# Two layers of a bidirectional hybrid diffusion trunk on one core: the framework's scheduler orders each engine's instructions by its timeline simulation

## The chip, the cores and the metric

The kernel runs on one core of a Trainium2 chip (trn2). The metric is the device time of one launch in microseconds (us), the median of several runs. A core has TensorE (PE: matmuls; its weight loads are shown apart as PEld), VectorE (DVE), ScalarE (ACT), GpSimd (POOL) and SyncE (SP, which here issues the loads and stores). Each engine works through its own list of instructions in order; an instruction whose inputs are not there holds up all that stand behind it on its engine.

## The reference

One inference step of a trunk of two layers, model width 1024, on 128 context tokens and 512 latent tokens, all in fp32. Each layer is a half-step SwiGLU feed-forward, a token mixer and a second half-step feed-forward. Every part has an RMSNorm before it and shift, scale and gate vectors made from a conditioning vector (`mod_w`, nine blocks of 1024 x 1024 per layer):

```python
for i in range(DEPTH):
    m = (jax.nn.silu(cond) @ mod_w[i] + mod_b[i]).reshape(cond.shape[0], N_MOD, 1, D_MODEL)
    h = rmsnorm(x, norm_g[i, 0]) * (1.0 + m[:, 1]) + m[:, 0]
    x = x + 0.5 * m[:, 2] * swiglu(h, f1a[i], f1b[i])
    h = rmsnorm(x, norm_g[i, 1]) * (1.0 + m[:, 4]) + m[:, 3]
    if i % 2 == 0:
        y, s_a, s_b = mix_even(h, s_a, s_b, is_latent, even)
    else:
        y, s_a, s_b = mix_odd(h, s_a, s_b, odd)
    x = x + m[:, 5] * y
    h = rmsnorm(x, norm_g[i, 2]) * (1.0 + m[:, 7]) + m[:, 6]
    x = x + 0.5 * m[:, 8] * swiglu(h, f2a[i], f2b[i])
return rmsnorm(x, final_norm), new_states
```

`mix_even` is retention (four heads, chunks) beside a gated linear recurrence (RG-LRU); `mix_odd` is an S5 state-space layer beside RWKV-7. Each mixer runs over the tokens in both directions and has one input and one output projection.

## The kernel before, in words

The activations lie transposed: eight tiles `x[d]` of 128 channels by 640 tokens, worked on in two halves h of 320 columns (h=0 and h=1; h=1 holds 192 latent and 128 context columns, so what depends on the conditioning is two instructions there). A product in fp32 is made of three matmuls (`mm3`, L414 to L416) of a high and a low part: high by high, high weight by low data, low weight by high data. So every weight is loaded raw (L376, SP's queue), cast to its high part on ScalarE (`whi`, L377) and subtracted for its low part on VectorE or, for a few, GpSimd (`wlo`, L378). Two weights are in flight (`wp`, bufs=2).

The stages follow each other as f01, m0, f02, f11, m1, f12 and fin: feed-forward 1 of layer 0, its mixer, feed-forward 2, and so on.

- `ffn`: 22 blocks f of 128 hidden units, in groups of 7, 7, 6 and 2. For each block, `up` makes gate and value in four PSUM banks ("gu"), then L548 (Silu), L549 (product) and a split (L401, L402). After each of the first three groups an **output pass** follows: 16 accumulator groups of 21 or 18 matmuls (four weights times two channel tiles times two halves), in two PSUM banks ("acc"). `add_res` (L506, VectorE) adds each to `x` and so frees its bank: one instruction for h=0, two for h=1.
- The last group of two blocks is `last_pass`, a **joint** between stages: its releases (L506) go together with the next norm's squares (L441 to L445), its statistics (`stat`: L450 on TensorE, L453 to L460) and `apply`: L482 (VectorE), L487 (ScalarE, high part), L488 (VectorE, low part). The next stage's first matmuls read what L487 and L488 write; h=0 is applied inside `last_pass`, h=1 after the first h=0 matmuls of the next stage.
- `mod_steps` makes the modulation vectors: per block eight tiles `mw` of 128 x 1024 (L297, SP's queue), each multiplied into two sums on VectorE (L331 for the first tile, L333 for the others), and then small matmuls (L338). `extra()` puts two or three such steps after each hidden block and each weight of the output pass, above all in f01 and f11. Two first blocks are made on TensorE in the start (`first_mods`, L306 loads, L309 matmuls).
- `load_in_slots` (L385) loads the first weight of the next stage in four tiles; L392 and L393 split it on ScalarE and GpSimd.
- `mix0` has the recurrence's gate matmuls (L741) with their activations (L742, L744, L745, L756) beside retention heads; `mix1` has small matmuls of 64 columns (L1520) in chains with VectorE (L1594 to L1693), and projections (L1133 to L1410) between them.

The code's order is not the order on the engines. The program is written down as a whole, and on leaving the `TileContext` the framework's scheduler gives every engine its list. It keeps the dependences, and chooses among instructions that are ready by estimates of when each engine would be free and how long things take. With no argument it uses its default machine model for these estimates. The programs' names carry numbers (`mw_328`, `s_251`), by which one tile can be followed in both orders.

## Time and profile before

| what | us |
|---|---|
| median of 3 runs (lowest to highest) | 2984.92 (2982.17 to 2988.34) |
| profiled execution | 2976.69 |
| its span in the profile | 2974.9 |
| TensorE busy | 2824.3 |
| VectorE busy | 1774.9 |
| ScalarE busy | 970.5 |
| GpSimd busy | 267.1 |

The profiled execution is one run of its own, 1.8 us of it outside the span. Busy times are summed over the span. Windows give them stretch by stretch, with the number of instructions in parentheses; `PEclk` there is the clock granted to TensorE as a mean share of full speed, between its levels of 1.2 and 2.4 GHz. A wait is put down to the instruction that released it last.

### The profile page before, as it was taken

How to read it: one execution, taken by the hardware profiler on the slowest of the kernel's cores; microseconds unless marked ns; L12 is line 12 of the kernel's file. 1: busy time of each engine (PE TensorE's matmuls, PEld its weight loads, DVE VectorE, ACT ScalarE, POOL GpSimd, SP SyncE). 2: the span in 40 equal slices, each digit the busy share in tenths (PEclk: the TensorE clock that was granted, in tenths of full speed). 3: DMA queues.
4: the chain of work that ended last, by engine and by line, in shares of the span. 5: the costliest groups of instructions: out<-in, count | busy, mean ns of one | idle time of the engine just before them, and what ended most of it. 6: DMA issues, size and time to landing. Idle time of an engine off the chain costs nothing.

```text
span 2974.9 us, 60269 instructions
## 1 busy us (share of the span) xinstructions
PE 2824.3 (95%) x25764; PEld 2672.6 (90%) x25764; DVE 1774.9 (60%) x3717; ACT 970.5 (33%) x1825; POOL 267.1 (9%) x214
## 2 busy tenths in 40 slices
PE   6999999999999999999999999988888998999997
PEld 4999999887899999999999998986777888999997
DVE  7585773875795475558456556486665537233335
ACT  4222123574442122224122214235443424222123
POOL 2000000140010000010000002212222102000001
PEclk8999999999999999999999999998989999999999
DMA  7464543211223343443335443341000112222221
GB/s 280 133 199 134 185 149 119 93 43 57 90 78 96 102 123 109 152 152 103 113 120 159 131 156 103 116 149 40 5 5 13 45 44 71 66 84 66 84 71 64
DMA packets 121965, 305.27 MB, mean 103 GB/s; under 512 B 20832, under 2 KB 38880, under 8 KB 121568
## 3 DMA queue, kind: packets, MB, share of 16 engines
q1 hardware_dynamic: 121696, 301.42, 31.4%
q8 instruction: 202, 3.31, 0.5%
q14 instruction: 67, 0.55, 0.1%
HBM read 276.95 MB, written 24.42 MB: 101 GB/s over the span
## 4 chain that ended last, share of the span: by engine, by line
PE 80%; DVE 9%; issue 6%; ACT 2%; POOL 2%; DMA 1%; SPq 0%; DVEq 0%; ACTq 0%; POOLq 0%
PE gu L415 17%; PE gu L414 17%; PE gu L416 17%; PE acc L414 7%; PE acc L416 7%; PE acc L415 7%; PE m L1520 2%; PE acc L1520 1%; PE gu L1520 1%; DVE s L445 1%; DVE s L402 1%; DVE t L482 1%; PE gu L1184 1%; DVE s L506 1%; DVE ma L333 1%
## 5 line engine op out<-in xcount | busy, mean ns | idle before, releaser
L414 PE MATMUL gu<-s,whi 128*128 128x320 f32 x3344 | 1040.6, 312 | 1.3 <-ACT s L1270 1.3
L415 PE MATMUL gu<-s,whi 128*128 128x320 f32 x3344 | 1036.0, 310 | 0.0
L416 PE MATMUL gu<-s,wlo 128*128 128x320 f32 x3344 | 1035.5, 310 | 0.0
L414 PEld LDWEIGHTS gu<-s,whi 128*128 128x128 f32 x3344 | 628.7, 188 | 8.5 <-issue 3.4
L415 PEld LDWEIGHTS gu<-s,whi 128*128 128x128 f32 x3344 | 628.9, 188 | 3.3 <-issue 1.4
L416 PEld LDWEIGHTS gu<-s,wlo 128*128 128x128 f32 x3344 | 628.4, 188 | 0.9
L377 ACT CAST whi<-raw 128x1024 fp32r<-128x1024 f32 x322 | 316.8, 1000 | 788.6 <-PE acc L415 444.1
L414 PE MATMUL acc<-s,whi 128*128 128x320 f32 x1456 | 452.0, 310 | 6.3 <-DVE s L506 6.2
L416 PE MATMUL acc<-s,wlo 128*128 128x320 f32 x1456 | 451.2, 310 | 0.0
L415 PE MATMUL acc<-s,whi 128*128 128x320 f32 x1456 | 450.2, 309 | 0.0
L549 DVE TENSOR_TENSOR t<-t,gu 128x320 f32<-128x320 f32 x176 | 85.5, 487 | 521.9 <-PE gu L416 517.6
L378 DVE TENSOR_TENSOR wlo<-raw,whi 128x1024 fp32r<-128x1024 f32 (+2 forms) x298 | 342.5, 1164 | 61.6 <-ACT whi L377 61.6
L414 PEld LDWEIGHTS acc<-s,whi 128*128 128x128 f32 x1456 | 273.3, 188 | 11.7 <-DVE s L506 8.8
L333 DVE SCALAR_TENSOR_TENSOR ma<-mw,cT,ma 128x1024 f32<-128x1024 f32 x224 | 277.2, 1278 | 0.0
L416 PEld LDWEIGHTS acc<-s,wlo 128*128 128x128 f32 x1456 | 273.2, 188 | 0.8 <-DVE wlo L378 0.4
L415 PEld LDWEIGHTS acc<-s,whi 128*128 128x128 f32 x1456 | 273.3, 188 | 0.2 <-issue 0.2
L506 DVE SCALAR_TENSOR_TENSOR s<-acc,hg,s 128x320 f32<-128x320 f32 (+1 forms) x336 | 137.5, 435 | 218.5 <-PE acc L416 217.3
L401 ACT CAST s<-t 128x320 fp32r<-128x320 f32 x212 | 96.4, 455 | 323.5 <-DVE t L549 323.2
L548 ACT ACTIVATE t<-gu 128x320 f32<-128x320 f32 x176 | 76.7, 438 | 312.7 <-PE gu L416 312.6
L393 POOL TENSOR_TENSOR s<-s,s 128x512 fp32r<-128x512 f32 x28 | 38.9, 1418 | 1477.6 <-DVE s L402 1337.7
L402 DVE TENSOR_TENSOR s<-t,s 128x320 fp32r<-128x320 f32 x212 | 110.4, 521 | 33.8 <-ACT s L401 33.7
L414 PE MATMUL gu<-s,s 128*128 128x320 f32 x304 | 92.2, 338 | 30.3 <-ACT s L487 28.7
(426 smaller groups left out, 3519.7 us busy)
## 6 DMA issues: line engine op xcount, KB each, us to landing
raw<-w SPq DMA_DIRECT2D x224, 512.0 KB, 3.9
mw<-mod_w SPq DMA_DIRECT2D x144, 512.0 KB, 4.4
raw<-w_in SPq DMA_DIRECT2D x36, 512.0 KB, 3.6
raw<-w SPq DMA_DIRECT2D x32, 384.0 KB, 4.1
xs<-s SPq DMA_DIRECT2D x16, 320.0 KB, 2.2
s<-xs SPq DMA_DIRECT2D x16, 320.0 KB, 5.3
s<-w SPq DMA_DIRECT2D x16, 256.0 KB, 5.5
raw<-w SPq DMA_DIRECT2D x16, 256.0 KB, 3.7
```

The source lines that it names most:

```text
L333: DVE.scalar_tensor_tensor(acc[s], w, cT[:, k, s:s + 1], acc[s], ALU.mult, ALU.add)
L377: ACT.copy(hi[:, c], raw[:, :n])
L378: (eng or DVE).tensor_sub(lo[:, c], raw[:, :n], hi[:, c].bitcast(F32))
L401: (DVE.tensor_copy if eng is DVE else ACT.copy)(hi, src)
L402: DVE.tensor_sub(lo, src, hi.bitcast(F32))
L414: PE.matmul(ps, whi, xhi, start=start, stop=False)
L415: PE.matmul(ps, whi, xlo, start=False, stop=False)
L416: PE.matmul(ps, wlo, xhi, start=False, stop=stop)
L506: DVE.scalar_tensor_tensor(x[d][:, c0 + a:c0 + b], ps[:, a:b], g[:, d, s:s + 1], x[d][:, c0 + a:c0 + b], ALU.mult, ALU.add)
L548: ACT.activation(sg, pg, AF.Silu)
L549: DVE.tensor_mul(gf, sg, pu)
L1520: PE.matmul(out(rows[h]), lhs(rows[h], h), rhs(rows[h], h), start=i == 0, stop=i == len(terms) - 1, tile_position=(64 * h, 64 * h))
```

## The change

```diff
-    with tile.TileContext(nc) as tc:
+    with tile.TileContext(nc, schedule_with_timeline_sim=True) as tc:
         build(nc, tc, I, O)
```

The scheduler takes its estimates from the framework's timeline simulation and no longer from its default machine model. The same instructions result, with the same tiles, but for the table loads of ScalarE, which are put in wherever the next activation needs another table: 51 before, 67 now. On every engine the order differs in most stages; f12 is nearly the same. Three places:

SP's queue in the start, from the middle of the `first_mods` loads on (`mw` from `mod_w`: L306, and L297 for VectorE's mod work; `s_251` to `s_254`: the first feed-forward weight; `raw`: later weights). Before:

```order
L306 DMA mw_328<-mod_w 128x2x512
L385 DMA s_251<-w_1 128x512
L385 DMA s_252<-w_1 128x512
L385 DMA s_253<-w_1 128x512
L385 DMA s_254<-w_1 128x512
L306 DMA mw_334<-mod_w 128x2x512
L306 DMA mw_340<-mod_w 128x2x512
L306 DMA mw_346<-mod_w 128x2x512
L376 DMA raw_558<-w_1 128x1024
L376 DMA raw_562<-w_1 128x1024
L297 DMA mw_806<-mod_w 128x1024
L297 DMA mw_810<-mod_w 128x1024
```

Now:

```order
L306 DMA mw_322<-mod_w 128x2x512
L376 DMA raw_682<-w_1 128x1024
L306 DMA mw_328<-mod_w 128x2x512
L306 DMA mw_334<-mod_w 128x2x512
L376 DMA raw_686<-w_1 128x1024
L306 DMA mw_340<-mod_w 128x2x512
L306 DMA mw_346<-mod_w 128x2x512
L297 DMA mw_806<-mod_w 128x1024
L385 DMA s_251<-w_1 128x512
L385 DMA s_252<-w_1 128x512
L385 DMA s_253<-w_1 128x512
L385 DMA s_254<-w_1 128x512
```

The weight tiles of L385 went behind the last of the `first_mods` loads, two raw weights and one `mw` of L297.

VectorE near the end of the second output pass of f01 (`acc_…` are the accumulator groups, in order of their numbers; `ma` are the mod sums). Before:

```order
L378 TENSOR_TENSOR wlo_3360<-raw_3361,whi_3359 128x1024
L378 TENSOR_TENSOR wlo_3360<-raw_3365,whi_3359 128x1024
L506 SCALAR_TENSOR_TENSOR s_116<-acc_3265,hg_0_1432,s_116 128x320
L333 SCALAR_TENSOR_TENSOR ma_3126<-mw_3487,cT,ma_3126 128x1024
L435 SCALAR_TENSOR_TENSOR ns_2_7705<-mod_7_3014,vec 128x16
L506 SCALAR_TENSOR_TENSOR s_116<-acc_3288,hg_0_1432,s_116 128x192
L506 SCALAR_TENSOR_TENSOR s_116<-acc_3288,hg_0_1432,s_116 128x128
L506 SCALAR_TENSOR_TENSOR s_118<-acc_3312,hg_0_1432,s_118 128x320
L506 SCALAR_TENSOR_TENSOR s_118<-acc_3335,hg_0_1432,s_118 128x192
```

Now:

```order
L506 SCALAR_TENSOR_TENSOR s_116<-acc_3265,hg_0_1432,s_116 128x320
L333 SCALAR_TENSOR_TENSOR ma_3632<-mw_3769,cT,ma_3632 128x1024
L506 SCALAR_TENSOR_TENSOR s_116<-acc_3288,hg_0_1432,s_116 128x192
L506 SCALAR_TENSOR_TENSOR s_116<-acc_3288,hg_0_1432,s_116 128x128
L333 SCALAR_TENSOR_TENSOR ma_3631<-mw_3773,cT,ma_3631 128x1024
L333 SCALAR_TENSOR_TENSOR ma_3632<-mw_3773,cT,ma_3632 128x1024
L333 SCALAR_TENSOR_TENSOR ma_3631<-mw_3777,cT,ma_3631 128x1024
L333 SCALAR_TENSOR_TENSOR ma_3632<-mw_3777,cT,ma_3632 128x1024
L333 SCALAR_TENSOR_TENSOR ma_3631<-mw_3905,cT,ma_3631 128x1024
L506 SCALAR_TENSOR_TENSOR s_118<-acc_3312,hg_0_1432,s_118 128x320
```

Between the release of `acc_3288` and that of `acc_3312` stood nothing, and now five L333 stand there. From the pass's first L506 to its last there were 16 L333, 2 L331 and 8 L378 and are now 30, 4 and 6. In f01's first pass L333 went from 19 to 26, in f11's second from 12 to 26, in f02's third from 12 to 4.

VectorE at the joint of f02 and f11, from the statistics of h=0 (L458 to L460) to the first L488 of its apply (`s_7293` to `s_7307` are x, `wlo_13892` is the next stage's second weight, of which the two instructions come some 20 rows later in the order before). Before:

```order
L458 TENSOR_TENSOR t_13431<-t_13430 128x320
L506 SCALAR_TENSOR_TENSOR s_7301<-gu_13513,hg_2_9358,s_7301 128x192
L459 TENSOR_TENSOR t_13431<-t_13431,t_13429 128x320
L506 SCALAR_TENSOR_TENSOR s_7301<-gu_13513,hg_2_9358,s_7301 128x128
L460 SCALAR_TENSOR_TENSOR s_13314<-t_13431,t_13430 128x320
L506 SCALAR_TENSOR_TENSOR s_7303<-acc_13525,hg_2_9358,s_7303 128x192
L482 SCALAR_TENSOR_TENSOR t_13439<-s_7293,ns_0_13315,s_13314 128x320
L482 SCALAR_TENSOR_TENSOR t_13445<-s_7295,ns_0_13315,s_13314 128x320
L482 SCALAR_TENSOR_TENSOR t_13451<-s_7297,ns_0_13315,s_13314 128x320
L488 SCALAR_TENSOR_TENSOR s_13438<-t_13439,mod_0_3922,s_13437 128x320
```

Now:

```order
L506 SCALAR_TENSOR_TENSOR s_7307<-acc_13549,hg_2_9358,s_7307 128x128
L459 TENSOR_TENSOR t_13431<-t_13431,t_13429 128x320
L378 TENSOR_TENSOR wlo_13892<-raw_13893,whi_13891 128x1024
L460 SCALAR_TENSOR_TENSOR s_13314<-t_13431,t_13430 128x320
L378 TENSOR_TENSOR wlo_13892<-raw_13897,whi_13891 128x1024
L482 SCALAR_TENSOR_TENSOR t_13439<-s_7293,ns_0_13315,s_13314 128x320
L482 SCALAR_TENSOR_TENSOR t_13445<-s_7295,ns_0_13315,s_13314 128x320
L482 SCALAR_TENSOR_TENSOR t_13451<-s_7297,ns_0_13315,s_13314 128x320
L482 SCALAR_TENSOR_TENSOR t_13465<-s_7301,ns_0_13315,s_13314 128x320
L482 SCALAR_TENSOR_TENSOR t_13471<-s_7303,ns_0_13315,s_13314 128x320
L482 SCALAR_TENSOR_TENSOR t_13477<-s_7305,ns_0_13315,s_13314 128x320
L488 SCALAR_TENSOR_TENSOR s_13438<-t_13439,mod_0_3922,s_13437 128x320
```

Releases of h=1 and the two splits went ahead of the first L482, and three more L482 ahead of the first L488. The joints of f01 to m0 and f11 to m1 changed in the same way.

## Rows read from the trace of the kernel before

**Rows 1.** Page, its first line and section 1: span, busy us of each engine.

```profile
span 2974.9 us, 60269 instructions
...
PE 2824.3 (95%) x25764; PEld 2672.6 (90%) x25764; DVE 1774.9 (60%) x3717; ACT 970.5 (33%) x1825; POOL 267.1 (9%) x214
```

**Rows 2.** Windows: stretch, its us, busy (x instructions) per engine, PEclk, DMA share, GB/s.

```profile
300.00:350.00 50.00, 50.00 (x351) 49.11 (x350) 47.94 (x60) 9.20 (x12) 0.00 (x0) 1.00 0.70 217
600.00:650.00 50.00, 46.89 (x264) 41.25 (x262) 39.16 (x64) 36.95 (x63) 18.93 (x15) 0.97 0.12 43
2040.00:2100.00 60.00, 48.25 (x534) 30.67 (x534) 42.04 (x83) 34.88 (x59) 22.41 (x17) 0.83 0.10 29
2100.00:2200.00 100.00, 88.69 (x2366) 78.53 (x2364) 65.66 (x162) 42.65 (x111) 31.28 (x25) 0.86 0.02 4
2370.00:2460.00 90.00, 78.58 (x1244) 71.01 (x1241) 36.24 (x80) 24.79 (x60) 10.49 (x9) 0.95 0.24 75
2600.00:2650.00 50.00, 50.00 (x343) 50.00 (x342) 17.84 (x30) 8.74 (x11) 0.00 (x0) 1.00 0.24 82
```

**Rows 3.** Waits of TensorE, whole span: waiting line, releaser, total us, times, longest us.

```profile
PE gu L414 <- ACT s L487: 28.7, 13, 4.6
...
PE acc L414 <- DVE s L506: 7.0, 7, 2.3
...
PE m L741 <- ACT s L742: 5.3, 5, 2.6
```

**Rows 4.** Start: two windows, then SP's and TensorE's timeline (start us, us, instruction, wait).

```profile
30.00:35.00 5.00, 0.42 (x9) 0.09 (x1) 4.80 (x8) 3.49 (x8) 3.06 (x3) 1.00 1.05 386
35.00:40.00 5.00, 5.00 (x33) 2.23 (x34) 4.58 (x4) 1.31 (x4) 3.83 (x3) 0.66 0.96 381
...
23.13 1.88 SPq L385 DMA_DIRECT2D s<-w  x4
...
34.92 0.48 PE L414 MATMUL gu<-s,s 128*128 128x320 f32 x1 [4.58 <-ACT s L487]
```

**Rows 5.** Timeline of VectorE in the second output pass of f01.

```profile
316.01 1.22 DVE L378 TENSOR_TENSOR wlo<-raw,whi 128x1024 fp32r<-128x1024 f32 x1
317.14 0.55 DVE L506 SCALAR_TENSOR_TENSOR s<-acc,hg,s 128x320 f32<-128x320 f32 x1
317.61 0.95 DVE L378 TENSOR_TENSOR wlo<-raw,whi 128x768 fp32r<-128x768 f32 x1
...
320.70 1.42 DVE L331 TENSOR_SCALAR ma<-mw,cT 128x1024 f32<-128x1024 f32 x2 [0.39 <-PE m L338]
...
324.96 2.47 DVE L333 SCALAR_TENSOR_TENSOR ma<-mw,cT,ma 128x1024 f32<-128x1024 f32 x2
327.36 0.67 DVE L506 SCALAR_TENSOR_TENSOR s<-acc,hg,s 128x192 f32<-128x192 f32 x2
327.94 2.08 DVE L378 TENSOR_TENSOR wlo<-raw,whi 128x1024 fp32r<-128x1024 f32 x2
```

**Rows 6.** Joint of f02 and f11: timeline of VectorE; TensorE's waits, 1335 to 1400.

```profile
1343.86 2.03 DVE L482 SCALAR_TENSOR_TENSOR t<-s,ns,s 128x320 f32<-128x320 f32 x3
1345.81 0.54 DVE L488 SCALAR_TENSOR_TENSOR s<-t,mod,s 128x320 fp32r<-128x320 f32 x1
...
1353.50 1.23 DVE L378 TENSOR_TENSOR wlo<-raw,whi 128x1024 fp32r<-128x1024 f32 x1
...
PE gu L414 <- ACT s L487: 3.8, 2, 2.3
```

**Rows 7.** Timeline of ScalarE in mix0: a table load between two activations.

```profile
595.34 0.88 ACT L783 ACTIVATE t<-gu 64x320 f32<-64x320 f32 x2
596.24 1.28 ACT L756 ACT_TABLE_LOAD   x1
597.53 0.74 ACT L756 ACTIVATE s<-s 128x640 f32<-128x640 f32 x1
```

**Rows 8.** Waits of SP's queue, whole span.

```profile
SPq L297 <- DVE ma L333: 215.9, 94, 5.7
```

## The prediction

> **What bounds the kernel now.** I read the page's totals first. TensorE is busy 2824.3 of 2974.9 us and every other engine far less [rows 1], so the end moves only if TensorE comes to wait for longer, or shorter, than the 150.6 us for which it stands idle now. The profiled execution took 2976.7 us, 8.2 us under the median of 2984.9 us; I make the sum against the profiled one and add it to the median at the end. The windows say next where the idle time lies. In the feed-forward stages TensorE has none, 343 matmuls and 50.00 us in a window of 50, even where VectorE is busy 47.94 us of it [rows 2]. The idle time sits in the mixes (46.89 of 50 us at 600 us in mix0; 48.25 of 60, 88.69 of 100 and 78.58 of 90 us in three stretches of mix1), in the start, and at the joints between stages. The waits of TensorE name who ended it: at the joints and the start ScalarE's part of a norm's apply (L487, 28.7 us in 13 waits), in the feed-forward output passes VectorE's release of an accumulator (L506, 7.0 us), in mix0 the gate activations (L742, 5.3 us) [rows 3]. The change adds no arithmetic; it reorders. So I look for places where the new order puts other work of an in-order engine ahead of what TensorE needs next.
>
> **1. Start: +8 us.** All loads go through SP's one queue. From 30 to 35 us the DMA engines are full (share 1.05, 386 GB/s) and to 40 us nearly so (0.96) [rows 4]. In the new order six transfers of 128 x 1024 floats stand newly ahead of the first feed-forward weight tiles s_251 to s_254 (mw_334, mw_340, mw_346, raw_682, raw_686, mw_806): 3.15 MB by 0.386 MB per us is 8.1 us. These tiles were issued at 23.13 us before, and the first feed-forward matmul ran at 34.92 us, after a wait of 4.58 us for L487 and not for the weights [rows 4]. So the weights may have had up to a few us of slack, which gives a lower end of 4; the same weights still have to be split by ScalarE and GpSimd, and VectorE's mod work (L331, L378) now stands ahead of the norm's L482, which gives 12 at the upper end. I take 8, the queue's own arithmetic, since TensorE has nothing else to run there.
>
> **2. Output passes of f01 and f11: +13 us.** An output pass is 16 accumulator groups; 21 matmuls at 50 us per 343 [rows 2] make 3.07 us each, so 15 groups between VectorE's first and last release are 46.0 us. There are two accumulator banks, so VectorE may lag by about one group and no more. Back to back (start to start) VectorE takes 1.20 us for an L333 (two from 324.96 to 327.36), 0.47 us for an L506 of 320 columns (317.14 to 317.61), 0.58 us for the pair of 192 and 128 (327.36 to 327.94), 1.13 us for a wlo split of 1024 columns (316.01 to 317.14), and 0.71 us for an L331 (two in 1.42) [rows 5]. The splits of 768 columns I count like those of 1024. Before, the second pass of f01 holds 16 L333, 2 L331 and 8 splits between first and last L506: 19.2 + 1.4 + 9.0 + 8.4 for the releases, 38.0 us, and the trace shows TensorE full there [rows 2]. In the new order it holds 30 L333, 4 L331 and 6 splits: 36.0 + 2.8 + 6.8 + 8.4 = 54.0 us, 8.0 over the budget. The first pass of f01 and the second of f11 go to 26 L333 (from 19 and 12), 2 L331 and 6 splits: 31.2 + 1.4 + 6.8 + 8.4 = 47.8 us, 1.8 over each. That is 11.6 us by totals. It isn't spread evenly: in one place five L333 (6.0 us) stand between two releases, where a group takes 3.07, which costs up to 3 us on top each time; against that, work before the first and after the last release hides up to a group's time per pass. Bounds: 4 and 22. I take 13, near the totals, with a little for the bunches. Where the mod work leaves, nothing is saved, as TensorE was full there and VectorE had time to spare.
>
> **3. Joints between stages: +13 us.** At the joint f02 to f11 VectorE runs back to back from the last pass's releases through the statistics to the apply: three L482 from 1343.86, the first L488 at 1345.81, and the two wlo splits of the next weight only from 1353.50 on [rows 6]. TensorE waits 3.8 us for L487 in two waits there, the longest 2.3 us (so 1.5 and 2.3, h=0 and h=1) [rows 6]. The new order puts both splits (2.3 us) and the five remaining releases of h=1 (1.4 us) before the first L482, and six L482 (three more, 2.0 us at 0.65 each) before the first L488. The first L482 is 3.7 us later and the first L488 over 5 us later; the first L450 comes after fewer matmuls on TensorE, which gains nothing as VectorE is the one that is full. Of these 5 us, about 2.5 come back, since h=0 starting late takes away the wait of h=1, whose statistics are no later than before. That makes 2.5 us each at f01 to m0 and f11 to m1, and 3 at the two joints around f02. At f02 to f11 three L333 and two L331 stand besides among the apply of h=1 (about 5 us), so there nothing comes back: 5 us in all, 13 for the four. f12's joint has no split to move: 0. Bounds: 5 (everything made up while h=0 runs) and 20. One row raises the upper end: after the start's 4.58 us wait the granted clock of the next 5 us was 0.66 [rows 4], between the levels of 1.2 and 2.4 GHz; 0.34 of 5 us is 1.7 us. Four such waits would be another 7. The Trainium skill ("TensorE: Matmul & The Clock Gate", section "Why this matters for your kernels") says the same, that a gap between bursts of matmuls brings the half clock back; by it these 7 us belong in the sum, and it would be 38 where mine is 31.
>
> **4. mix0: -3 us.** TensorE's L741 groups stand further apart, with up to 32 projection matmuls between two of them where 15 stood, so the 5.3 us of waits for L742 [rows 3] can go. Against that ScalarE gets ten more table loads, because the square root (L756) is done per head and no longer per pair: 10 by 1.28 us = 12.8 us [rows 7] on an engine that is busy 36.95 of 50 us [rows 2]. In the row the load costs no more than its 1.28 us: the work before it ends at 596.22 and the next activation starts at 597.53. It can hide, as ScalarE has 13 us spare in each 50. The Trainium skill ("ScalarE: Activation LUTs", "What ACT_TABLE_LOAD costs") adds a drain and puts a switch at 2.66 us; by that figure, an estimate, ten cost 26.6 us, more than the spare time of two such windows, and this term would be about +5. The row shows no drain, so I keep -3; bounds -5 and +8.
>
> **5. mix1: 0.** Here nearly every row moves. Projection and key matmuls that filled TensorE between the links of the small-matmul chain are pulled ahead of early chains and missing in late ones, and six more table loads (7.7 us) come. No row prices this. The most that could be won is the idle time, 11.75 + 11.31 + 11.42 = 34.5 us in the three stretches [rows 2], and what the clocks of 0.83 and 0.86 cost there, 0.17 of 60 and 0.14 of 100 us, 24 us together. A loss of half that size is as easy. I put 0 with -25 and +20.
>
> The steady part of f12 and the end keep their order: 0. Sum: 8 + 13 + 13 - 3 + 0 = **+31 us**: 3007.7 for an execution like the profiled one, and 2984.9 + 31 = **3016 us** as a median.
>
> **Rivals.**
> *mix1 pays (faster).* The chain's waits and its low clock hold 58.5 us. If the new interleaving takes more than 37 of these, the sum falls under -6: say two thirds, 39 us, which gives 2984.9 + 31 - 39 = 2977. For it: the stretch has the largest idle time of the program, and the new order does pull independent matmuls forward. Against: what fills early gaps is missing in later ones, and the chain's own links (VectorE to TensorE and back) don't get shorter by order. 0.13; with half of the 58.5 us the change comes out at 0, within 0.2% (6 us, what a measurement of this kernel can tell from no change): 0.08.
> *VectorE's crowding is harmless.* The windows show TensorE full with VectorE at 96% [rows 2]. If the passes absorb all but 4 us and the joints cost 5 to 9, it is 8 + 4 + 9 - 3 = 18: 3003. 0.20.
> *The crowding cascades.* SP already waits 94 times for L333 to free a mod tile, 215.9 us in all [rows 8], and the next feed-forward weights stand behind it in the same queue. If bunched L333 make each of a pass's four weights late by such a wait (2.3 us on average), the three crowded passes lose 9 us each on top: 31 + 28 = 59, or 3044. 0.14.
> That the change does nothing is excluded by the two orders.
>
> **Numbers.** Forecast 0.45, and with the two slower rivals 0.79 for slower; 0.08 for the same; 0.13 for faster. The range leaves out about 0.1 of the faster case and the far end of the cascade: 2979 to 3047. The slower cases alone span 2995 to 3047.
>
> **What will show it.** Right: the first feed-forward matmul at 42 to 43 us instead of 34.92; TensorE waits for L506 up from 7.0 to about 20 us, in the windows of the second passes of f01 and f11; waits for L487 up from 28.7 to about 45 us, the single ones at joints 4 to 6 us; ScalarE's table loads 67 in place of 51; f12 as long as before. Wrong: mix1 shorter by over 20 us with fewer waits at L1520 (first rival), L506 waits unchanged (second), or TensorE waiting for weight splits or for DMA inside f01 and f11 (third).

## The result, and the profile after

| | before | changed |
|---|---|---|
| median, us (lowest to highest) | 2983.55 (2978.91 to 2988.34) | 3060.55 (3059.85 to 3062.92) |
| profiled execution, us | 2976.69 | 3059.85 |

Four runs of each; the ratio is 1.026 (95 % interval 1.0246 to 1.0274). The change makes the kernel slower by 77 us, where I forecast 31 and ended the range at 3047. The sign was right, the size less than half. The two profiled executions, from whose traces the places below are read, lie 83 us apart, since before's was 6.9 us under its median.

The page of the changed kernel, its span and engines, beside [rows 1]:

```profile
span 3058.1 us, 60327 instructions
...
PE 2842.9 (93%) x25764; PEld 2688.8 (88%) x25764; DVE 1783.6 (58%) x3717; ACT 987.7 (32%) x1841; POOL 277.7 (9%) x214
```

The span is 83.2 us longer. TensorE is busy for 18.6 us more with the same 25764 matmuls, and idle for 215.2 us instead of 150.6. Its waits, beside [rows 3] (columns as there):

```profile
PE gu L414 <- ACT s L487: 40.1, 10, 5.9
PE acc L414 <- DVE s L506: 20.9, 19, 9.9
PE m L1520 <- DVE ys L1632: 19.4, 19, 4.5
PE gu L415 <- DVE s L488: 16.7, 10, 3.7
...
PE m L741 <- ACT s L742: 2.2, 1, 2.2
```

L506, L487 and the waits for L488 (3.9 us before) grow; L742 falls from 5.3 to 2.2.

To put the 83 us in their places I matched the two traces at equal TensorE work: the **lag** at a point is how much later the changed kernel has got through the same columns of matmuls. The lag is 83.1 us from f12's first blocks on and 81.6 us at the last matmul. A stretch's cost is the growth of the lag across it:

| place | predicted | in the changed kernel | in a run of its own |
|---|---|---|---|
| start | +8 | +6.6 | +6.4 (h_bodies) |
| output passes of f01, f11 | +13 | +10.8 | +10.8 (h_bodies) |
| output passes of f02 | 0 | +7.1 | +5.7 (h_bodies) |
| the four joints | +13 | +31 | +30.4 (h_joints) |
| f12's joint | 0 | +6.6 | +6.8 (h_joints) |
| mix0 | -3 | +13 | +11.5 (h_bodies) |
| mix1 | 0 | +8 | +10 (m1_all) |
| f12 and the end | 0 | -1.5 | -1.5 (h_bodies) |
| sum | +31 | +81.6 | +80 |

The last column comes from the experiments below. Its parts add up to the whole within 2 us, and each agrees with its place within 2 us: the places hardly act on each other, so each can be taken alone.

**The start** went as forecast, beside [rows 4]. The timeline of SP's queue, changed kernel:

```profile
32.57 2.95 SPq L385 DMA_DIRECT2D s<-w  x4
```

That of TensorE, at the first feed-forward matmul:

```profile
44.22 0.90 PE L414 MATMUL gu<-s,s 128*128 128x320 f32 x2 [2.81 <-ACT s L487]
```

ScalarE's, just ahead of the L487 that ends this wait:

```profile
41.07 2.64 ACT L392 CAST s<-s 128x512 fp32r<-128x512 f32 x4 [0.40 <-DMA s<-w]
```

And the window in which it falls (columns as in [rows 2]):

```profile
40.00:45.00 5.00, 1.65 (x8) 0.79 (x4) 4.48 (x7) 4.14 (x8) 3.24 (x3) 0.50 1.05 407
```

The tiles of L385 are issued 9.4 us later (32.57, before 23.13), with the DMA engines full (1.05), and the first matmul runs at 44.22 instead of 34.92. The row of ScalarE joins the two: its casts of these tiles (L392) wait for their landing and begin at 41.07, where they began at 32.24 and waited for no load before, and L487 stands behind them in ScalarE's list.

**The joint of f02 and f11**, beside [rows 6]. VectorE's timeline, changed kernel:

```profile
1389.49 0.48 DVE L453 TENSOR_SCALAR t<-m 128x320 f32<-128x320 f32 x1
...
1392.06 1.22 DVE L378 TENSOR_TENSOR wlo<-raw,whi 128x1024 fp32r<-128x1024 f32 x1
...
1393.60 1.22 DVE L378 TENSOR_TENSOR wlo<-raw,whi 128x1024 fp32r<-128x1024 f32 x1
1394.74 4.07 DVE L482 SCALAR_TENSOR_TENSOR t<-s,ns,s 128x320 f32<-128x320 f32 x6
1398.73 1.47 DVE L488 SCALAR_TENSOR_TENSOR s<-t,mod,s 128x320 fp32r<-128x320 f32 x3
```

TensorE's timeline there:

```profile
1386.90 0.81 PE L450 MATMUL m<-s,ones 128*128 128x320 f32 x2 [0.24 <-DVE s L445]
...
1390.53 0.31 PE L416 MATMUL acc<-s,wlo 128*128 128x320 f32 x1
1396.73 0.90 PE L414 MATMUL gu<-s,s 128*128 128x320 f32 x2 [5.89 <-ACT s L487]
```

The splits (L378) and all six L482 stand ahead of the first L488, as the orders said. TensorE gets its last matmul of the old stage at 1390.53 and then stands for 5.89 us, where it stood for 1.5. Counted from h=0's L453, its next stage begins at +7.2 us (1396.73 against 1389.49); before it began at +5.1, by its rows on TensorE and VectorE:

```profile
1339.70 0.81 PE L450 MATMUL m<-s,ones 128*128 128x320 f32 x2 [1.11 <-DVE s L445]
...
1345.67 0.56 PE L414 MATMUL gu<-s,s 128*128 128x320 f32 x2 [1.50 <-ACT s L487]
```

```profile
1340.55 0.48 DVE L453 TENSOR_SCALAR t<-m 128x320 f32<-128x320 f32 x1
```

Three windows of the changed kernel from the end of the old stage on (columns as in [rows 2]):

```profile
1391.00:1397.00 6.00, 0.27 (x1) 0.27 (x2) 6.00 (x11) 3.15 (x5) 2.38 (x2) 0.69 0.39 126
1397.00:1407.00 10.00, 8.84 (x43) 8.44 (x44) 8.07 (x17) 5.54 (x14) 0.54 (x1) 0.67 0.08 30
1407.00:1417.00 10.00, 9.52 (x73) 8.55 (x71) 4.17 (x10) 3.96 (x8) 1.83 (x2) 1.00 0.01 2
```

And two of before that answer to the second and third, from its first matmuls of the next stage on:

```profile
1345.00:1355.00 10.00, 9.29 (x61) 9.04 (x62) 9.99 (x23) 7.82 (x18) 0.88 (x1) 1.00 0.01 2
1355.00:1363.00 8.00, 6.88 (x55) 5.91 (x53) 6.04 (x12) 3.41 (x7) 1.69 (x2) 1.00 0.42 134
```

After the wait, TensorE works the next 10 us at a granted clock of 0.67, two thirds of them at 1.2 GHz; before, both windows behind the wait of 1.5 us were at 1.00. Summed over the trace, TensorE is granted 1.2 GHz for 218 us instead of 127 (the spans' mean granted clocks are 0.964 and 0.979).

**mix0** has one wait of 9.9 us. TensorE's timeline:

```profile
828.03 0.63 PE L414 MATMUL acc<-s,whi 128*128 128x320 f32 x1 [9.91 <-DVE s L506]
```

VectorE's, at the L506 that it waits for:

```profile
821.53 1.25 DVE L929 TENSOR_SCALAR s_xq<-s_xq 128x32 f32<-128x32 f32 x1
...
822.82 1.21 DVE L933 TENSOR_TENSOR s_mag<-s_xq,s_mi 128x32 f32<-128x32 f32 x1
...
825.33 1.25 DVE L966 TENSOR_TENSOR s_ar<-s_mag,s_cs 128x32 f32<-128x32 f32 x1
826.50 0.18 DVE L967 TENSOR_TENSOR s_ai<-s_mag,s_sn 128x32 f32<-128x32 f32 x1
...
827.33 0.18 DVE L943 TENSOR_TENSOR s5rho<-s5rho 128x32 f32<-128x32 f32 x1
827.43 1.12 DVE L506 SCALAR_TENSOR_TENSOR s<-acc,mod,s 128x320 f32<-128x320 f32 x3
```

GpSimd's, at the same time:

```profile
821.35 5.18 POOL L393 TENSOR_TENSOR s<-s,s 128x512 fp32r<-128x512 f32 x4 [118.54 <-ACT s L392]
```

And the window ahead of it:

```profile
797.00:827.00 30.00, 21.12 (x139) 20.37 (x137) 28.36 (x96) 15.44 (x26) 5.18 (x4) 0.94 0.36 125
```

Before, this L506 ran at 796.84 us. With the lag of 23 us that the changed kernel has there it would run at 820; it runs at 827.43, and the lag grows by 9.4 us within the next ten. From 797 to 827 VectorE is busy 28.36 of 30 us: it isn't waiting for anything but working through what stands ahead of L506: the last head's steps and, from 812 us on, almost only the S5 preparation (L921 to L1095), which is for mix1. Four of these instructions of 32 columns take 1.21 to 1.25 us, one during each of GpSimd's four L393, where their like take 0.17 to 0.19 us beside them. By these rows some 4.3 us of the 9.9 are this slowing, an estimate (four times 1.06); the rest is the queue itself.

### The profile page after: what moved, and what is told of

Its sections match the earlier page's. It is cut to its first block, busy times and chain, and to the rows that moved or that the text cites. A ratio compares the mean times of both kernels' runs of the same rounds, so it can differ in the third digit from the quotient of the medians.

```text
span 3058.1 us, 60327 instructions
## 1 busy us (share of the span) xinstructions
PE 2842.9 (93%) x25764; PEld 2688.8 (88%) x25764; DVE 1783.6 (58%) x3717; ACT 987.7 (32%) x1841; POOL 277.7 (9%) x214
## 3 DMA queue, kind: packets, MB, share of 16 engines
q1 hardware_dynamic: 121696, 301.42, 30.4%
## 4 chain that ended last, share of the span: by engine, by line
PE 58%; DVE 10%; issue 4%; ACT 2%; POOL 2%; DMA 1%; SPq 0%; DVEq 0%; ACTq 0%; POOLq 0%
PE gu L415 12%; PE gu L416 12%; PE gu L414 12%; PE acc L414 5%; PE acc L415 5%; PE acc L416 5%; PE acc L1520 2%; PE m L1520 2%; DVE ma L333 2%; DVE s L506 1%; PE gu L1520 1%; DVE t L482 1%; DVE s L445 1%; DVE wlo L378 1%; DVE s L402 1%
## 5 line engine op out<-in xcount | busy, mean ns | idle before, releaser
L377 ACT CAST whi<-raw 128x1024 fp32r<-128x1024 f32 x322 | 307.1, 999 | 763.5 <-PE acc L415 465.5
L378 DVE TENSOR_TENSOR wlo<-raw,whi 128x1024 fp32r<-128x1024 f32 (+2 forms) x298 | 341.6, 1173 | 37.5 <-ACT whi L377 37.3
L333 DVE SCALAR_TENSOR_TENSOR ma<-mw,cT,ma 128x1024 f32<-128x1024 f32 x224 | 280.0, 1283 | 0.0
L506 DVE SCALAR_TENSOR_TENSOR s<-acc,hg,s 128x320 f32<-128x320 f32 (+1 forms) x336 | 136.9, 435 | 204.0 <-PE acc L416 203.4
L393 POOL TENSOR_TENSOR s<-s,s 128x512 fp32r<-128x512 f32 x28 | 38.8, 1417 | 1489.6 <-DVE s L402 1359.3
L402 DVE TENSOR_TENSOR s<-t,s 128x320 fp32r<-128x320 f32 x212 | 105.9, 501 | 36.5 <-ACT s L401 36.4
```

The source lines that it names most:

```text
L333: DVE.scalar_tensor_tensor(acc[s], w, cT[:, k, s:s + 1], acc[s], ALU.mult, ALU.add)
L377: ACT.copy(hi[:, c], raw[:, :n])
L378: (eng or DVE).tensor_sub(lo[:, c], raw[:, :n], hi[:, c].bitcast(F32))
L402: DVE.tensor_sub(lo, src, hi.bitcast(F32))
L506: DVE.scalar_tensor_tensor(x[d][:, c0 + a:c0 + b], ps[:, a:b], g[:, d, s:s + 1], x[d][:, c0 + a:c0 + b], ALU.mult, ALU.add)
```

## The experiments

Except where fills are named, every kernel here holds the same instructions as before, each engine's list pinned by edges that order two neighbours and carry no wait. A diff shows how the list was put together: "before" is before's order, and "new" gives stretches (us of before's trace) whose instructions stand in the changed kernel's order; the numbers themselves are left out. Where the `us` of a single execution stands alone, before ran beside it on the same chip, at 2977.9 to 2986.9. A lag is one profiled execution's; in stretches of mix1 whose order was before's it drifted by up to 8 us (m0_l506_xs), at the joint of f11 and m1 by 3.5 (m1_all, m0_l506_xs), elsewhere mostly by 1 to 2. Between the moved stretches it stays flat: in h_joints it is 15.0 us from 885 to 1327 us of before. So the pinning itself costs nothing there that the lag shows.

**1. h_joints: only the five joints in the new order** (four executions).

```diff
+new = [(518, 575), (838, 885), (1327.5, 1375), (1816, 1865), (2465.5, 2515)]
 order = pin(before, new)
```

> Every engine's order is pinned: the order of the kernel before, but in five stretches of 45 to 57 us around the joints (f01-m0, m0-f02, f02-f11, f11-m1, m1-f12) the new order. Theory A (the new order at the joints makes TensorE wait 4 to 6 us for the apply of h=0, and after such a wait the granted clock is at 1.2 GHz for some 10 us in place of 0 to 3.4): 35 to 42 us over before, the matmul work lagging 6 to 10 us per joint, low clock 10 us at each. Theory B (the joints cost the 13 us of the prediction; the rest of the 83 us is work that comes late from the bodies of the stages and only shows at the joints): 10 to 16 us over before.

3019.84 us, ratio 1.0121 (1.0102 to 1.014). The joints cost 4.6, 10, 10.1, 5.7 and 6.8 us of lag. The waits of TensorE in it:

```profile
PE gu L414 <- ACT s L487: 40.9, 11, 5.9
...
PE gu L415 <- DVE s L488: 14.9, 11, 3.7
PE acc L414 <- DVE s L506: 10.5, 16, 2.3
```

The same two waits grow as in the changed kernel, without anything of the stages between. So the joints alone carry 37 us, where I had 13.

**2. h_bodies: all the rest, without mix1** (one execution).

```diff
-new = [(518, 575), (838, 885), (1327.5, 1375), (1816, 1865), (2465.5, 2515)]
+new = [(0, 518), (575, 838), (885, 1327.5), (1375, 1816), (2515, end)]
```

> The complement, without mix1: the order of the kernel before in the five joints and in mix1, the new order in the start, f01, the body of mix0, f02, f11 and f12. Theory A: 30 to 40 us over before: start 9, passes of f01 4, mix0 13, f02 4, f11 5. Theory B: 55 to 65 us over before.

3012.11 us; lag 35.4 through f12 and 33.9 at the last matmul. Start 6.4, passes of f01 5.7, mix0 11.5, passes of f02 5.7 and of f11 5.1.

**3. What makes a joint dear?** Its edits were taken apart in four runs (one execution each): j_nosplit puts the two splits back behind the apply; splits_xs has only the splits (and their casts) early; cover_m1d is the joint with splits and the order of L482 and L488 as before, which leaves TensorE's order and the releases; second_m1a has only the second half of the joint, the apply of h=1, in the new order. Three of them carry an edit in mix0 or mix1 besides, which the lag keeps apart.

```diff
 joint = new order of VectorE, ScalarE, TensorE, SP, GpSimd
-L378 x2, L482 x6, L488, ...          # j_nosplit
+L482 x6, L488, ..., L378 x2
-L482 x3, L488, ..., L378 x2          # splits_xs, from before's order
+L378 x2, L482 x3, L488, ...
-L378 x2, L482 x6, L488, ...          # cover_m1d
+L482 x3, L488, ..., L378 x2
+new = [(549.5, 575), (867.3, 885), (1357.7, 1375), (1846.3, 1865), (2497.1, 2515)]   # second_m1a
```

> As the first run, but VectorE's two wlo splits (L378) go back behind the apply of h=0 at four joints (the fifth has none). If the two splits ahead of the first L482 are what makes the wait long (2.3 of 3.7 us): the wait for L487 falls by 2.3 us per joint, and 12 to 20 us of the first run's excess go, more than 9 because the clock stays up. If it is the six releases and the six L482 in a row: under 6 us go.

> Pinned to the order before, with two things of the new order, in places that don't touch. At four joints only the two wlo splits (and their casts) go ahead of the first L482, nothing else. If the splits make the wait: L487's wait at h=0 is 2.3 us longer at each, 8 to 14 us in all with the clock. If they are a side issue beside the releases and the TensorE order: 4 to 8 us. In the body of mix0 the new order, but SP issues the eight reloads of x (L278) ahead of the two raw weights that stand in front of them: in the h_bodies run mix0 cost 11.5 us, of which a 9.9 us wait for the first L506 of the output projection. If the reload's place in SP's queue makes that wait, mix0 costs 2 to 4 us here; if VectorE's S5 preparation makes it (it delays what frees x's tiles), it stays at 9 to 12.

> At the five joints the new order, but with the splits behind the apply of h=0 and the L482 and L488 of h=0 among themselves as before: what is left of the change there is the order of releases, squares and TensorE's matmuls, and the apply of h=1. If the lost cover is what costs (the statistics' matmul L450 has 12 matmuls behind it in place of 25, about 1.9 us less work for TensorE while VectorE and ScalarE make the apply): the h=0 wait stays at 3 to 4.5 us in place of 1.5, and the joints cost 22 to 30 of their 38 us. If the six L482 in a row cost: under 15. In mix1, from 2070 to 2415 us of before, the new order in all engines: 20 to 29 us if the new interleaving of the chain is what costs there, under 8 if mix1's loss in the changed kernel only came from the state in which it was entered.

> At the joints the order before up to the statistics of h=1, and only the apply of h=1 in the new order. If the L331 and L333 (f11) and the S5 preparation (f02) among the apply of h=1 cost time by themselves: 3 to 5 us at each of these two joints, 0 to 1 at the other three, 7 to 12 in all. If they only cost because h=0 came late: 0 to 3 in all. In mix1 the new order from 1870 to 2070 us, where the changed kernel had caught up 8 to 12 us: the same gain here, and if the joints cost little, the whole kernel at or under the time before.

| run | us | wait of TensorE for h=0 | cost of the five joints, us |
|---|---|---|---|
| before | | 1.5 (f12 3.1) | 0 |
| h_joints | 3019.84 | 5.9 (f12 3.5) | 37 |
| j_nosplit | 3012.51 | 4.3 | 34 |
| splits_xs | 3012.16 | 4.5 | 18 (four) |
| cover_m1d | 3029.48 | 4.3 | 28 |
| second_m1a | 2996.38 | 1.5 | 21 |

No part alone is the cause, and the costs of the parts don't add. Without the splits the wait is still 4.3 us, and the splits alone make 4.5. Two things lengthen the wait without the splits. On TensorE, 13 matmuls more of `last_pass` stand ahead of h=0's L450 in the new order, so that 12 follow it where 25 did, 1.9 us less to fill the wait with. And on VectorE releases of h=1 (L506) stand ahead of L453. TensorE's rows in cover_m1d:

```profile
1350.13 0.81 PE L450 MATMUL m<-s,ones 128*128 128x320 f32 x2 [0.24 <-DVE s L445]
...
1358.39 0.90 PE L414 MATMUL gu<-s,s 128*128 128x320 f32 x2 [4.32 <-ACT s L487]
```

VectorE's:

```profile
1352.73 0.48 DVE L453 TENSOR_SCALAR t<-m 128x320 f32<-128x320 f32 x1
```

From L450 to the next stage's first matmul it is 8.3 us here, 9.8 in the changed kernel and 6.0 before. Of the 2.3 us more, 1.75 lie between L450 and L453 (2.60 against 0.85 us). No run parts the lost cover from these releases. The six L482 in a row don't lengthen this wait: with them (j_nosplit) and without (cover_m1d) it is 4.3 us. But L488 stands behind them, and TensorE's waits for it come to 14.4 us in j_nosplit and 6.6 in cover_m1d, whose joints are 6 us cheaper. second_m1a moves nothing of h=0 and still costs 3 to 6 us at a joint. At f01 to m0 and f11 to m1 that need not be the new order: before's own order drifted by 3.5 us at the latter. At f02 to f11, where it costs 6.1, L331 and L333 stand on VectorE among the apply of h=1, and TensorE has a new wait:

```profile
PE gu L415 <- DVE s L488: 4.1, 1, 4.1
```

My expectation for it (at most 12 us in all) was too low, as it was for splits_xs; and j_nosplit gained 3 us of the joints' lag where the splits, as the sole cause, would have given 12 to 20.

**4. Does the half clock cost by itself?** a_fill24 and a_fill44 are the changed kernel with 24 and 44 unread matmuls of 320 columns ahead of the first real matmul of each of the six stages f01, m0, f02, f11, m1 and f12; nothing else moves. (The mixers' first matmuls are projections, so b_fill16's "six feed-forward stages", below, are these six too.)

```diff
+    def fill(ps, w0):
+        group = [PE.matmul(ps, w0.hi[1][:, :P], w0.hi[0][:, :HALF], start=True, stop=True) for _ in range(24)]
...
+                if together and h == 0:      # feed-forward
+                    fill(pg, w)
...
+                if i == 0 and h == 0:        # mixer
+                    fill(ps[0], n.w0)
```

> The new order everywhere, and 24 matmuls of 320 columns that nobody reads (3.5 us at full clock) ahead of the first real matmul of each stage, written into a bank that the real matmul starts anew. They fill the wait for L487. Theory A, second half (the wait brings the clock down, and the low clock costs about half of its duration): low clock at the joints falls from 10 to 0 to 4 us each, and the kernel gets 12 to 20 us faster than the changed one, 60 to 70 us over before. Rival (the time at the joints is the wait itself, the clock is only a sign of it): no gain, or up to 5 us loss.

> The new order with 44 unread matmuls of 320 columns (6.4 us) ahead of each stage's first real one, which reach to the end of the wait for L487, where 24 left 2.4 us of it open and the clock still fell. If the low clock at the joints costs time: low clock falls to 0 to 3.4 us a joint and the joints get 2 to 4 us shorter each, 8 to 16 in all against the changed kernel. If VectorE's and ScalarE's apply sets the pace there, so that TensorE at half clock still keeps up: 0, or a loss of up to 3 us as the filling ends late.

a_fill24 (four executions): 3056.8 us, 1.0243 of before (1.022 to 1.0266). That is 4 us under the changed kernel, whose interval (1.0246 to 1.0274) it overlaps, and 1.3 us in the lag; I'd expected 12 to 20 if the clock costs. a_fill44 (one execution): 3047.32. TensorE's waits of a_fill24 at the joint of f02 and f11 (L495 is L487 of before, eight lines up):

```profile
PE gu L422 <- ACT s L495: 4.0, 2, 2.4
```

Its windows behind that joint (columns as in [rows 2]):

```profile
1395.00:1405.00 10.00, 6.67 (x27) 6.27 (x28) 9.79 (x20) 6.98 (x16) 2.21 (x2) 0.66 0.29 102
1405.00:1415.00 10.00, 10.00 (x69) 9.84 (x68) 3.49 (x8) 3.09 (x5) 1.48 (x2) 1.00 0.00 1
```

And those of a_fill44:

```profile
1395.00:1405.00 10.00, 9.32 (x62) 9.16 (x63) 7.41 (x17) 5.21 (x12) 0.00 (x0) 1.00 0.01 4
1405.00:1415.00 10.00, 6.85 (x54) 5.78 (x53) 6.70 (x14) 6.35 (x16) 2.75 (x3) 1.00 0.00 0
```

With 24 a gap of 2.4 us is left at h=0, and the 10 us behind it are at 0.66 again. With 44 that gap is gone and the clock stays at 1.00. The five joints then cost 2.4, 0.6, 1.8, 2.1 and 1.4 us less than in the changed kernel, 8.3 in all. The lag at the end is 12.5 us smaller, though the fill makes this kernel's start 1 us later; the remaining gain lies in stretches between the joints, where nothing was filled, and is of the size of their drift. Of the joints' 37 us, about a fifth is thus the clock that the fill gives back.

**5. b_fill16: before's order with 16 such matmuls** (ten executions).

```diff
+        group = [PE.matmul(ps, w0.hi[1][:, :P], w0.hi[0][:, :HALF], start=True, stop=True) for _ in range(16)]
```

> Before's order (pinned), with 16 unread matmuls of 320 columns put on TensorE ahead of the first gate/up matmul of each of the six feed-forward stages. Before's own waits there are 4.6 us at the start and 1.5 us (3.1 at f12) at the joints, and 3.4 us at 1.2 GHz follow at three of the five. If the half clock there costs by itself: low clock at the joints 0 to 3.4 us and a gain of 2 to 6 us, so 0.998 to 0.9993 of before. If the waits alone are the cost, or the fill is itself in the way (16 take 2.1 us at 2.4 GHz, where 1.5 us are waited): no gain or a loss of up to 5 us.

2979.45 against 2983.23 us, ratio 0.9991 (0.9979 to 1.0002): no difference that can be told. Before's own gaps aren't worth filling so. No run here clearly beat before.

**6. mix0.** Five tries at mending the new order of mix0 by hand gained nothing. splits_xs put the reload of x (L278) ahead of two raw loads in SP's queue; m0_prep2 moved the S5 preparation behind the other work of 785 to 821 us; m0_both did both. m0_l506 and m0_l506_xs put the first three L506 ahead of the preparation too.

```diff
 SP:  -L376 raw x2, L278 s<-xs x8        +L278 s<-xs x8, L376 raw x2             # splits_xs, m0_both, m0_l506_xs
 DVE: -L905..L1110 between L402, L879    +L402, L879, ..., then L905..L1110      # m0_prep2, m0_both, m0_l506, m0_l506_xs
 DVE: -L905..L1110, L506 x3              +L506 x3, L905..L1110                   # m0_l506, m0_l506_xs
```

> Before's order, with mix0's body (575 to 838 us of before) in the new order, in which the lines 905 to 1110 (the preparation of the S5 scans, on VectorE, ScalarE and TensorE) that the new order runs at 785 to 821 us are moved behind the other work of these 36 us. If that preparation, standing ahead of the last head's output on VectorE, makes mix0's loss (11.5 us in the bodies' run, 10.8 us with the x reload earlier in SP's queue): mix0 costs 2 to 5 us and the run about 2986. If the loss comes from what is before 785 us or after 821 us in the new order: mix0 still costs 9 to 12 us, the run about 2995.

> As m0_prep2 (before's order, mix0's body in the new order, the S5 preparation of 785 to 821 us moved behind the other work), and besides SP issues the x reload (L278, 8 transfers) ahead of the two raw loads (L376) that stand before it in the new order. In m0_prep2 VectorE's splits of the last head's output (L402), whose tiles the reload takes, came 11 to 14 us earlier than in the run with the reload moved alone, but SP stood 20 us at the raws, which wait for a split (L378). If each of the two by itself holds the reload: TensorE's longest wait for L506 falls from 20.8 us to under 4 and mix0 costs 2 to 6 us, the run about 2987. If something else holds the reload or TensorE: it still costs 10 us or more.

> As m0_prep2, but the first three L506 on VectorE now stand ahead of the moved S5 preparation instead of behind it; SP's order as in the new order, so the reload (L278) comes behind the two raws (in m0_prep2 at 800.7 us, landing 6 to 8 us after its issue). If VectorE's in-order queue held L506: the wait falls from 20.8 us to 6 to 12, what the late reload leaves, and mix0 costs 6 to 13 us. If the reload alone sets it, or something else: no change against m0_prep2, about 22 us.

> As m0_l506, with the reload ahead of the two raws in SP's queue (in m0_both it was issued from 783.5 to 797.4 us). If the two together made the wait (the preparation ahead of L506 on VectorE, the reload behind the raws on SP): the wait for L506 is under 4 us, and mix0 costs 0 to 6 us. If not: 10 us or more.

mix0 cost 10.8 (splits_xs), 22 (m0_prep2), 22.6 (m0_both), 21 (m0_l506) and 24 us (m0_l506_xs): no better, or twice as dear. The block of the preparation went from between VectorE's splits to a place directly ahead of the first L506, and in the last two to one between the third and the fourth; wherever it stands in one piece, an L506 stands behind it, and TensorE's longest wait for L506 is 20.8, 20.7, 11.4 and 13.9 us in these four. The reload's place is ruled out by itself: in splits_xs it goes early, and the wait is still 9.9 us. So I cut mix0 by time instead:

```diff
+new = [(575, 745)]   # m0_head
+new = [(745, 783)]   # m0_mid
+new = [(783, 838)]   # m0_late
```

> Before's order, with 575 to 745 us of before (the RG-LRU gates with the projections between them, and the first heads) in the new order. The prediction's -3 for mix0 was meant for this stretch: if it holds there, -3 to 0 us. If the swings that the lag showed there (+8 at 625 us, back to +3) are the new order's own: +2 to +5 us.

> Before's order, with 745 to 783 us of before (the last head and its gates) in the new order. If the late last head makes the late output passes: 6 us or more by itself. If not: under 3 us.

> Before's order, with 783 to 838 us of before (output passes of mix0 beside the S5 preparation) in the new order; on VectorE the first L506 then stands behind 103 instructions of this stretch, where before 55 stood ahead of it. If VectorE's queue ahead of the first L506 makes mix0's loss: 6 to 11 us, with one wait for L506 of 6 to 11 us. If the loss needs the earlier parts too: under 4 us.

By the end of mix0, m0_head costs 3.3 us of lag, m0_mid 5.5 and m0_late 11.5. Within the stretches that moved it is less for the first two, 1.1 and 2.4; m0_mid lies between its two forecasts. The three together make 20 us, where the whole of mix0 in the new order costs 11.5, so parts of mix0 do act on each other. (What the lag gains later in these runs, 3 to 8 us, lies in stretches that didn't move.) m0_late has the very wait of the changed kernel, on TensorE:

```profile
809.64 0.64 PE L414 MATMUL acc<-s,whi 128*128 128x320 f32 x1 [9.90 <-DVE s L506]
```

Its VectorE:

```profile
808.95 0.18 DVE L943 TENSOR_TENSOR s5rho<-s5rho 128x32 f32<-128x32 f32 x1
809.05 1.12 DVE L506 SCALAR_TENSOR_TENSOR s<-acc,mod,s 128x320 f32<-128x320 f32 x3
```

And the window ahead of it:

```profile
784.00:809.00 25.00, 13.62 (x81) 12.90 (x79) 23.20 (x96) 8.96 (x16) 5.17 (x4) 0.83 0.35 122
```

VectorE is busy 23.20 of the 25 us ahead of it, with 103 instructions of this stretch in front of the first L506, where 55 stood before. So the release waits in VectorE's queue. As in the changed kernel four of the instructions of 32 columns take 1.21 to 1.25 us there, during GpSimd's L393 (802.97 to 808.14). Every engine's order moved in this stretch; VectorE's alone, and GpSimd's L393 elsewhere, were not tried. Before's order has the same preparation strewn among the L506. In m0_head the waits for L742 fall, as forecast, from 5.3 to 2.2 us, but its waits at the projections (L784 3.7, L786 1.8) are new. Its TensorE waits in mix0:

```profile
PE gu L414 <- DVE t L784: 3.7, 2, 2.6
PE m L741 <- ACT s L742: 2.2, 1, 2.2
...
PE gu L414 <- ACT s L786: 1.8, 1, 1.8
```

**7. m1_all: mix1 alone in the new order** (one execution).

```diff
+new = [(1870, 2440)]
```

> Before's order, with mix1 from 1870 to 2440 us of before in the new order and nothing else. In the changed kernel the lag grows by some 8 us between the joint into mix1 and f12's, beside swings of -11, +29 and -10; the prediction had 0, between -25 and +20. If mix1's own order makes that, whatever comes before it: 5 to 12 us, the run about 2991. If the 8 us come from the state in which the joints and mix0 leave the queues: under 4 us.

2991.56 us; the lag goes from 4.1 at the start of the stretch that moved to 14.1 behind mix1. That is 10.0, within what I expected if the order itself costs. (Another 3.5 came in the joint ahead, in before's order; the last section has its rows.) Inside it falls by 12 us to 2065 us and then grows by 32 to 2245. The waits of the chain, in this run:

```profile
PE m L1520 <- DVE ys L1632: 19.1, 18, 4.2
```

They were 9.0 us in 11 waits before. The stretch of 2070 to 2415 us alone cost 24 us in cover_m1d, and that of 1870 to 2070 alone gained 8 to 10 us in second_m1a but had given most of it back at 2090. That fits projections that are taken early and missing later in the same stage; no run moved them alone.

## Why the prediction was right or wrong

- **Start, +8: right** (6.6 to 9.3, by the point at which one measures). The arithmetic of the full queue held, and ScalarE's wait for the late tiles shows that it was the path.
- **Passes, +13: right in size, in part by luck.** f01 and f11 cost 10.8 us. The second pass of f01, 8.0 us over its budget, cost 3.2; f01's first and f11's second, 1.8 over each, cost 0.7 and 1.5. Another 3.9 are f11's first pass, whose 14 L333 did not change; why stays open. I expected waits at L506 of some 20 us in the second passes of f01 and f11; the total of 20.9 us was met by chance, as 9.9 of it is in mix0 and 4.9 at the four joints, and in f01 and f11 the waits are 2.7 us each. f02, which I put at nothing, cost 7.1, of it 3.7 at one place: a wait of 1.75 us for L402 and 3 us at a granted clock of 0.50 behind it.
- **Joints, +13: the step that failed most.** They cost 31. The wait for h=0 was forecast at 4 to 6 us and came out at 5.9, but I took its growth for the whole loss. By the end of h=0's part the lag has grown by 7.1, 9.7, 8.1 and 8.1 us at the four joints, where I had 5: besides the 4.4 us of the longer wait, TensorE waits 1.2 to 2.0 us for h=0's L488 and 1.1 to 1.6 for L506 at each, and runs at half clock behind it. "the first L450 comes after fewer matmuls on TensorE, which gains nothing" was a misreading: it comes after 13 more, only 12 are left behind it, and without the splits the wait is still 4.3 us (cover_m1d, j_nosplit). "Of these 5 us, about 2.5 come back" held at f01 to m0 and f11 to m1, where the lag falls by 2.2 and 2.4 us with h=1. It failed around f02: 0.2 us come back at m0 to f02, and at f02 to f11 another 2.8 are lost. The half clock behind the waits, which I put into the upper end at 7 us for four joints, was left out of the sum wrongly: filling the waits takes 6.9 us off these four (a_fill44). The Trainium skill ("TensorE: Matmul & The Clock Gate", section "Why this matters for your kernels"), by which those 7 us belonged in the sum, had the better of it: in the changed kernel each joint has 10.2 to 17.1 us at 1.2 GHz, where before had 0 to 3.4.
- **f12's joint, 0: wrong**, since I looked at splits alone. Six L482 stand ahead of its first L488 too, TensorE waits 2.5 us for L488 where it waited for none at h=0, and the joint costs 6.8 us (h_joints).
- **mix0, -3: wrong.** The gain at L742 came (3.1 us), and so did ScalarE's table loads, at no cost that a row shows by itself. The loss was on an engine I hadn't counted there: VectorE's 48 more instructions ahead of the first L506, 10 us of wait, some 4 of which are four of them slowed beside GpSimd's L393. I had worked out VectorE's work between releases for the feed-forward passes and not for mix0's, which has the same two banks. As for the table loads, the Trainium skill ("ScalarE: Activation LUTs", section "What ACT_TABLE_LOAD costs") has 2.66 us for a switch, load and drain together. A load takes 1.28 us here, as before, and its idle time in the row below is a wait for VectorE, so the trace shows no drain. ScalarE's line, changed kernel:

```profile
L756 ACT ACT_TABLE_LOAD x8 | 10.3, 1283 | 4.9 <-DVE s L751 4.9
```

- **mix1, 0: within its bounds** (8 in the changed kernel, 10 alone), and its rival, that it pays, is out. No row had priced it, so the 0 was a guess.
- **The cascade**, the rival nearest to the measured time, is not what happened: SP's waits for L333 went down, beside [rows 8]:

```profile
SPq L297 <- DVE ma L333: 203.2, 89, 6.6
```

The 51 us that were missing are so: joints 18, f12's joint 7, mix0 16, mix1 8, f02 7, less 5 at the start, the passes and the end. What stays open is which part of mix1's order costs its 8 to 10 us, and how the joints' 37 us split into h=0, h=1 and clock exactly, as the parts overlap.

## What to carry to other kernels

When an order moves work ahead of a release, add up what the in-order engine has between two releases in every stage with a small ring of banks, mixers as well as feed-forwards, and look for long blocks of tiny instructions that nobody needs soon, and at whether they keep their length beside the other engines' work. At a joint, count on the waiting engine how much of its own work still lies behind the instruction that starts the chain; that cover is worth as much as the chain's length. Let a delay "come back" only joint by joint, where a row shows the later part with slack.

## What was not expected of the hardware

At the joint of f02 and f11, TensorE's gap of 2.4 us was followed by 10 us at a granted clock of 0.66 (a_fill24), as much as its gap of 5.89 us (0.67, changed kernel); before's gap of 1.5 us there left the clock at 1.00. So filling more than half of the gaps gained 4 us of 3060 by the medians, within their noise, and filling them whole 13.

The length of a gap didn't decide it alone. At the joint of f11 and m1 in before's order, gaps of 1.51 and 2.6 us left the clock at 1.00 in one execution and were followed by half clock in another, with the same instructions in the same order. Before, behind the gap of 2.60 us:

```profile
1853.00:1864.00 11.00, 10.84 (x73) 10.50 (x73) 8.23 (x21) 6.90 (x18) 0.93 (x1) 1.00 0.01 1
```

m1_all, behind its gap of 2.61 us:

```profile
1854.00:1865.00 11.00, 10.80 (x54) 10.80 (x55) 6.90 (x18) 7.01 (x19) 1.31 (x2) 0.71 0.01 1
```

That joint cost m1_all 3.5 us. And VectorE's instructions of 32 columns took 1.21 to 1.25 us, one in each L393 of GpSimd, where others of 32 columns took 0.17 to 0.19.
